# Loading one of the last rows in six strided parts instead of five, meant to give the DMA engines 10, 9, 7 and 6 of its partitions

## The chip, the cores and the metric

The kernel runs on one core of a Trainium2 chip. The metric is the device time of one execution in microseconds (us). A trace, where one is quoted, is of one execution; "from the start" means from the start of its span. The kernel before took 162.47 us (median of 3 runs, 162.40 to 163.06).

## The reference

A log-sum-exp over the last axis of a 32 x 512 x 1024 array of float32:

```
x_max = np.max(x, axis=-1, keepdims=True)
return x_max.squeeze(-1) + np.log(np.sum(np.exp(x - x_max), axis=-1))
```

There are 16,384 rows of 1024 numbers, 67.1 MB to read and 64 KB to write. The kernel takes exp without subtracting the maximum, sums, and takes the logarithm. "Row" below means one row per partition: 128 x 1024 numbers, 512 KB. There are 128 such rows.

## The kernel before

The rows arrive in 17 loads, from 16 rows down to single ones. ScalarE takes exp of each load; VectorE sums most of them, ScalarE some with its own accumulator. The last four loads (13 to 16) are one row each and ScalarE sums all of them.

```
CHUNKS = [                       # rows, rows summed by VectorE, pieces, by halves
    (4, 4, 1, False), (15, 15, 1, False), (16, 16, 2, False), ...
    (5, 4, 1, True), (4, 3, 1, True), (3, 3, 1, False), (2, 2, 1, True),
    (1, 0, 1, False), (1, 0, 1, False), (1, 0, 1, False), (1, 0, 1, False),
]
UNEVEN = (13,)
PARTS = ((0, 128, 2), (1, 128, 4), (3, 128, 8), (7, 64, 8), (71, 128, 8))
...
        if i not in UNEVEN:
            nc.sync.dma_start(out=dst, in_=src).then_inc(landed[i], 16)
            return
        for first, last, step in PARTS:
            nc.sync.dma_start(
                out=dst[first:last:step], in_=src[first:last:step]
            ).then_inc(landed[i], 16)
...
        for j in range(n_dve, r):                    # rows that ScalarE sums
            nc.scalar.activation(out=ring[:, s + j], in_=ring[:, s + j], func=Exp,
                accum_out=total(row + j)).then_inc(act_done, 1)
```

Load 13, the row four from last, is thus fetched in five parts, each a strided set of partitions: 0, 2, 4, ...; 1, 5, 9, ...; and so on. Just ahead of the final row ScalarE also takes the logarithm of 43 finished sums.

The softmax here doesn't subtract the row's maximum and nothing guards it: scores larger than these inputs give would overflow.

## Time and profile before

| | kernel before |
|---|---|
| time, median of 3 | 162.47 us |
| bytes read, mean rate over the span | 67.11 MB, 417 GB/s |
| DMA queue, share of 16 engines' span | 97.4% |
| last update of the semaphores of loads 12 to 16, from the start | 153.03, 154.62, 155.68, 156.98, 158.22 us |
| first to last update of load 12; of load 16 (the stagger) | 0.68; 0.56 us |

A semaphore is a counter; ScalarE waits in the kernel until a full load has brought it to 16. The trace records 16 updates for such a load, each with its time, and the load has landed with the last of them. The page counts 16 DMA engines, and below each update is read as the end of one engine's share. That is the author's reading: no record of the trace gives an engine's number. The page and the chain tell which engine is busy; these records tell how close each wait is, also where no idle time is printed. The lines of the profile themselves are in the prediction.

### The profile page before, as it was taken

To read this page: it belongs to the slowest core of one execution; us is meant where nothing else is said; L and a number is where in the kernel's file an instruction comes from. 1 tells how busy PE (TensorE), PEld (TensorE's weight loads), DVE (VectorE), ACT (ScalarE), POOL (GpSimd) and SP (SyncE) were. 2 spreads that over 40 slices of the span, in tenths; PEclk is the share of its full clock that TensorE was granted. 3 is DMA by queue.
4 is the path that set the end of the run, shared out by engine and by line. 5 is a ranking of instruction groups with operands and counts; after the bars stand their busy time and mean duration, and the time that the engine had idled before them with its cause. 6 is when DMAs were issued, how large, how long until landed. Compare 5 with 4: busy or idle time off the path is not lost.

```text
span 161.2 us, 130 instructions
## 1 busy us (share of the span) xinstructions
DVE 121.0 (75%) x46; ACT 115.2 (71%) x40; POOL 0.2 (0%) x4
## 2 busy tenths in 40 slices
DVE  0028000003999999999999699999999999999891
ACT  3170006996089960999429993999199999999995
POOL 0000000000000000000000000000000000000000
DMA  7999799989989989989979999999999999999991
GB/s 256 508 488 442 335 442 520 407 374 520 423 358 520 423 358 520 423 358 520 423 325 455 455 455 439 423 423 423 404 412 439 455 427 406 426 423 421 405 386 49
DMA packets 2640, 67.18 MB, mean 417 GB/s; under 512 B 336, under 2 KB 464, under 8 KB 976
## 3 DMA queue, kind: packets, MB, share of 16 engines
q1 hardware_dynamic: 2640, 67.18, 97.4%
HBM read 67.11 MB, written 0.07 MB: 417 GB/s over the span
## 4 chain that ended last, share of the span: by engine, by line
DMA 49%; DVE 29%; ACT 20%; issue 1%
DMA ring<-in_x_dram 49%; DVE sums L168 29%; ACT ring L148 17%; ACT ring L175 3%; ACT res L119 0%
## 5 line engine op out<-in xcount | busy, mean ns | idle before, releaser
L168 DVE TENSOR_REDUCE sums<-ring 128x8 f32<-128x8192 f32 (+5 forms) x14 | 111.2, 7995 | 37.0 <-ACT ring L148 36.9
L148 ACT ACTIVATE ring<-ring 128x8192 f32<-128x8192 f32 (+6 forms) x18 | 104.4, 5837 | 43.6 <-DMA ring<-in_x_dram 43.5
L155 DVE CUSTOM_DVE_ANT_0 ring<-ring 128x512 f32<-128x512 f32 x16 | 9.9, 688 | 0.0
L175 ACT ACTIVATE ring<-ring 128x1024 f32<-128x1024 f32 x9 | 9.3, 1045 | 0.0
L133 ACT ACT_TABLE_LOAD x1 | 1.3, 1283 | 0.8 <-PEq L220 0.8
L175 ACT ACTIVATION_READ_ACCUMULATOR ring<-ring 128x1 f32 x9 | 1.6, 175 | 0.0
L155 DVE DVE_READ_ACCUMULATOR2_ANT sums<- 128x1 f32 x16 | 1.3, 84 | 0.0
L119 ACT ACTIVATE res<-sums 128x81 f32<-128x81 f32 (+1 forms) x2 | 0.5, 251 | 0.0
L119 ACT ACTIVATE res<-late 128x4 f32<-128x4 f32 x1 | 0.2, 174 | 0.0
L220 POOL MEMSET const-uint8-127<- 128x1 uint8 x1 | 0.1, 103 | 0.0
L220 POOL MEMSET const-bfloat16-1.0<- 128x1 bf16 x1 | 0.1, 102 | 0.0
L220 POOL MEMSET const-float32-0.0<- 128x1 f32 x1 | 0.1, 99 | 0.2 <-issue 0.2
L220 POOL MEMSET const-float32-1.0<- 128x1 f32 x1 | 0.1, 99 | 0.0
## 6 DMA issues: line engine op xcount, KB each, us to landing
ring<-in_x_dram SPq DMA_DIRECT2D x1, 7680.0 KB, 24.9
ring<-in_x_dram SPq DMA_DIRECT2D x1, 7168.0 KB, 28.6
ring<-in_x_dram SPq DMA_DIRECT2D x1, 6656.0 KB, 35.7
ring<-in_x_dram SPq DMA_DIRECT2D x1, 4608.0 KB, 20.2
ring<-in_x_dram SPq DMA_DIRECT2D x2, 2048.0 KB, 16.1
ring<-in_x_dram SPq DMA_DIRECT2D x1, 3584.0 KB, 28.3
ring<-in_x_dram SPq DMA_DIRECT2D x1, 2560.0 KB, 27.3
ring<-in_x_dram SPq DMA_DIRECT2D x1, 1536.0 KB, 28.0
```

The lines of the kernel that those rows point to most:

```text
L119: nc.scalar.activation(out=res[:, lo:hi], in_=src, func=Ln).then_inc(act_done, 1)
L133: nc.scalar.preload_act_table_set("natural_log_exp_and_others")
L148: nc.scalar.activation(out=ring[:, s + lo : s + hi], in_=ring[:, s + lo : s + hi], func=Exp).then_inc(act_done, 1)
L155: nc.vector.tensor_tensor_reduce(out=ring[:, s + j, : D // 2], in0=ring[:, s + j, : D // 2], in1=ring[:, s + j, D // 2 :], scale=1.0, scal ...
L168: nc.vector.reduce_sum(out=sums[:, row + lo : row + hi], in_=ring[:, s + lo : s + hi], axis=AX).then_inc(dve_done, 1)
L175: nc.scalar.activation(out=ring[:, s + j], in_=ring[:, s + j], func=Exp, accum_out=total(row + j),).then_inc(act_done, 1)
L220: nc = _bacc.Bacc("TRN2", target_bir_lowering=False, num_devices=1)
```

## The change

The updates of a load come one after another, those of load 12 within 0.68 us. The intent is to give the engines that are ahead more of one row, so that all finish the last loads together and the last landing comes earlier. The kernel before was meant to do it in two halves (9 and 7 partitions an engine), the change in four quarters (10, 9, 7, 6), by cutting the third part, 16 partitions, in parts of 12 and 4. Which engine moves which partitions is assumption.

```diff
-PARTS = ((0, 128, 2), (1, 128, 4), (3, 128, 8), (7, 64, 8), (71, 128, 8))
+PARTS = (
+    (0, 128, 2), (1, 128, 4), (3, 96, 8), (99, 128, 8), (7, 64, 8), (71, 128, 8),
+)
```

Nothing else changes; the program is the same up to the issue of this row at 128 us. Line numbers below the edit grow by two.

## The prediction

> **What bounds the kernel now.** I read the page first (busy shares, then the chain of work that ended last), then the chain in order of time, then the timeline of the last microseconds, and last a table of stretches.
>
> ```profile
> span 161.2 us, 130 instructions
> DVE 121.0 (75%) x46; ACT 115.2 (71%) x40; POOL 0.2 (0%) x4
> q1 hardware_dynamic: 2640, 67.18, 97.4%
> DMA 49%; DVE 29%; ACT 20%; issue 1%
> ```
>
> The DMA queue is moving packets during 97.4% of the span, and neither compute engine is over 75%. The kernel reads 67.11 MB once, so in bulk it is a stream of loads. What sets the end, though, is the last stretch, which the averages do not tell.
>
> ```profile
> 122.15 24.68 DMA ring<-in_x_dram
> 146.83 0.02 issue
> 146.85 2.77 ACT ring L148
> 149.62 1.04 ACT ring L175 x2
> 150.66 4.46 ACT ring L148 x2
> 155.12 3.02 ACT ring L175 x6
> 158.14 0.13 ACT res L119
> 158.27 0.00 ACT ring L175
> 158.27 0.94 issue
> ```
>
> The reader is to see that after 146.85 us the chain names no transfer any more: it is ScalarE, one row after another, to the end. The row that the change touches is the first of the final four; ScalarE takes each with one 128x1024 activation and its own sum. The timeline shows them:
>
> ```profile
> 155.03 1.04 ACT L175 ACTIVATE ring<-ring 128x1024 f32<-128x1024 f32 x1
> 156.03 1.05 ACT L175 ACTIVATE ring<-ring 128x1024 f32<-128x1024 f32 x1
> 157.03 1.05 ACT L175 ACTIVATE ring<-ring 128x1024 f32<-128x1024 f32 x1
> 158.03 0.24 ACT L119 ACTIVATE res<-sums 128x43 f32<-128x43 f32 x1
> 158.25 1.06 ACT L175 ACTIVATE ring<-ring 128x1024 f32<-128x1024 f32 x1
> ```
>
> Each row starts 1.00 us after the one before, with no idle time printed. Against this I set when the rows landed, from the trace's records of semaphore updates (16 per full transfer[...]; the last one opens the row). From the span's start the last updates of the four rows are at 154.62, 155.68, 156.98 and 158.22 us. ScalarE begins them at 155.03, 156.03, 157.03 and 158.25. So the slack of the transfers is 0.41, 0.35, 0.05 and 0.03 us: **the two streams end almost together.** The last row may even be a wait on its transfer: an earlier logarithm starts at 127.92 and the activation behind it at 128.09, 0.17 us later, while here the distance is 158.25 - 158.03 = 0.22 us. Without any wait for data the last row would have begun at about 158.20. Hence at most **0.05 us** can be won by landing the last rows earlier, and anything over some 0.03 us of delay is lost one for one.
>
> The uneven row is visible as a dip of the rate:
>
> ```profile
> 149.90:152.40 2.50, 2.49 (x10) 2.50 (x3) 0.00 (x0) 1.00 0.99 410
> 153.20:154.60 1.40, 1.25 (x1) 1.40 (x2) 0.00 (x0) 1.00 1.04 337
> 154.60:157.10 2.50, 2.50 (x2) 2.50 (x6) 0.00 (x0) 1.00 1.01 403
> ```
>
> The last two columns are the DMA engines' busy share and GB/s. The engines are as busy in the middle stretch, but move 337 GB/s, not 403 to 410; the 4096-byte packets take up to some 245 ns there, against 159 ns before and after, in the packet records. The five strided parts of this row cost about 1.4 x (1 - 337/410) = 0.25 us of streaming.
>
> [...]the row's semaphore has 66 records, two of them (131.54 and 132.20 us) just after the issues of the 8-partition parts.[...]
>
> **The change, part by part.** [...]all else stays, instruction for instruction on ScalarE and VectorE.
>
> 1. *Issue.* One more issue on SyncE's queue. The five cost 567 to 664 ns, median 592, so the next three rows are issued 0.6 us later, at 132.4 instead of 131.8 us. They land 24 to 25 us after their issue because the queue is full ahead of them. Effect on the end: 0.
>
> 2. *Bytes.* [...]One packet is 0.16 us[...].
>
> 3. *What it does to the last landing.* An ordinary load before this row lands over 152.35 to 153.03 us, a stagger of 0.68 us; after it the stagger is 0.54, and for the last row 0.56 us (157.66 to 158.22). The trace gives no engine numbers. I choose to assume that the stagger follows them: engines 0 to 3 first. The last row's sixteen updates are 157.66, .79, .87, .92; .98, 158.02, .03, .06; .07, .07, .16, .17; .18, .18, .21, .22. Adding 0.175 to the first four gives 157.83 to 158.10, taking 0.16 off the last four gives 158.02 to 158.06, the middle eight stay, and the last is now 158.17: 0.05 us earlier, and the stagger falls to some 0.2 to 0.35 us.
>
> 4. *What ScalarE makes of it.* It would begin the last row at 158.20 instead of 158.25. Sum: 0 + 0 - 0.05 = **-0.05 us**, 0.03% of 162.47.
>
> **Rivals.** *The skew is balanced the wrong way.* If one of the last engines in the list is among 0 to 3[...], its final landing goes from 158.22 to about 158.40, and the end moves by +0.15 us: about 162.6.[...] The dip costs 0.25 us now; if it grew by half the end would come 0.1 us later, if it shrank by half the landing would gain 0.12 us, of which ScalarE lets through only 0.05. *ScalarE hides it entirely.* If the last row was not waiting on data, the change is worth 0.00. *The new issue starves the queue*: it would take 20 us of delay, not 0.6; I give it nothing.
>
> **Range and chances.** The favourable end is cut off at -0.05 us; the unfavourable rivals give +0.1 to +0.2 us. Beside these stand the run-to-run differences of the kernel before, 162.40 to 163.06 us in three runs, which are larger than everything above. I expect 162.45 us, with 162.2 to 162.8 holding eight times in ten. Two per cent is 3.2 us, sixty times the gain that can be had and more than ten times the largest loss I can construct, so within 2% gets 0.98 and either side 0.01.
>
> **What would show it.** In the changed kernel's trace: the row's semaphore should have 64 + 4 = 68 records; six issues near 128.6 to 132.4 us; the stagger of the final row below 0.45 us; its last update between 158.1 and 158.2 us, and ScalarE's final activation about 0.17 to 0.2 us behind the logarithm of 43 columns, all relative to the same start of the stream. ScalarE's work from 116 us on should keep its durations. The prediction is wrong if the last update comes later than 158.3 us, if the stagger grows, or if the stretch of the uneven row falls well below 337 GB/s. A difference that lies before 128 us has nothing to do with the change.

The sum came to 0 + 0 - 0.05 = -0.05 us, and its last term, step 3, is an estimate on the assumption that the change gives four engines one packet more and four one packet less. A packet is 0.16 us in the trace before (159 ns), and 0.175 is that and 0.015 for a 4-byte packet of a semaphore update (9 ns there) with a gap. The count of 64 + 4 = 68 updates can be checked in the trace.

## The result, and the profile after

| | before | after |
|---|---|---|
| median, same rounds | 162.56 us (6 runs, 162.37 to 163.06) | 162.84 us (6 runs, 162.76 to 162.91) |
| ratio, 95% interval | | 1.0012 [0.9995, 1.0029]: the same at 2% |
| last updates of loads 12, 13, 14, 15, 16 | 153.03, 154.62, 155.68, 156.98, 158.22 | 153.20, 154.95, 156.04, 157.32, 158.56 |
| last landing of 12 to last landing of 16 | 5.19 us | 5.36 us |
| stagger of load 16 | 0.56 us | 0.66 us |

A ratio here is the mean time of one kernel's fast runs over that of the other's of the same rounds, so not quite the ratio of the medians.

The page of the changed kernel: the span, the busy times, the queue and the shares of the chain.

```profile
span 161.5 us, 131 instructions
DVE 121.0 (75%) x46; ACT 115.4 (71%) x40; POOL 0.2 (0%) x4
q1 hardware_dynamic: 2640, 67.18, 97.3%
DMA 48%; DVE 33%; ACT 13%; SPq 3%; issue 1%
```

The busy times and their shares are as they were; one more instruction is the sixth issue. The chain now holds 3% of SyncE's queue. In order of time (start, duration, what), its end is:

```profile
128.41 0.56 SPq L113
...
131.85 0.57 SPq L113
132.42 0.04 issue
132.47 0.44 SPq L108
132.91 0.04 issue
132.95 24.38 DMA ring<-in_x_dram
157.32 0.02 issue
157.35 0.81 ACT ring L177
```

The six issues stand in the chain only because a wait of ScalarE is now found at 157.32 us, for load 15, and the chain is followed from there back to that load's issue. The 24.38 us between issue and landing are the queue ahead of it (its packets take 97.3% of 16 engines' span), so the issues are not what cost anything. What matters is that the chain meets a transfer at 157.32, where before the last transfer in it ended at 146.83. ScalarE's own lines show both waits:

```profile
155.20 1.04 ACT L177 ACTIVATE ring<-ring 128x1024 f32<-128x1024 f32 x1
156.20 1.04 ACT L177 ACTIVATE ring<-ring 128x1024 f32<-128x1024 f32 x1
157.35 1.06 ACT L177 ACTIVATE ring<-ring 128x1024 f32<-128x1024 f32 x1
158.36 0.23 ACT L121 ACTIVATE res<-sums 128x43 f32<-128x43 f32 x1
158.59 1.06 ACT L177 ACTIVATE ring<-ring 128x1024 f32<-128x1024 f32 x1
```

The third row starts 1.15 us after the second, where the others follow at 1.00: 0.15 us of waiting for a landing at 157.32. The last starts 0.23 us after the logarithm, 0.02 us after its landing at 158.56. No idle time is printed for gaps as small as these; one sees them in the starts. The three stretches that the prediction shows, now of the changed kernel (last column GB/s):

```profile
149.90:152.40 2.50, 2.44 (x8) 2.50 (x3) 0.00 (x0) 1.00 0.98 413
153.20:154.60 1.40, 1.07 (x1) 1.40 (x2) 0.00 (x0) 1.00 1.06 310
154.60:157.10 2.50, 2.50 (x2) 2.50 (x4) 0.00 (x0) 1.00 1.01 405
```

The stretch of the strided row moves 310 GB/s instead of 337, with the engines just as busy (DMA share 1.06 against 1.04); ahead of it and behind it the rates are as before.

Of the 0.34 us between the two spans (161.18 and 161.52), 0.17 us are there at load 12 already, where the two programs are still the same. Over the twelve traces whose loads up to 12 come in undisturbed, that landing lies anywhere from 152.88 to 153.43 us, so this part is chance. The other 0.17 us lies behind it, and the experiments are about that part.

### The profile page after: what moved, and what is told of

Read it like the earlier page. It is cut to its first block, busy times and chain, and to the rows that moved or that the text cites. A ratio compares the mean times of both kernels' runs of the same rounds, so it can differ in the third digit from the quotient of the medians.

```text
span 161.5 us, 131 instructions
## 1 busy us (share of the span) xinstructions
DVE 121.0 (75%) x46; ACT 115.4 (71%) x40; POOL 0.2 (0%) x4
## 2 busy tenths in 40 slices
DMA packets 2640, 67.18 MB, mean 416 GB/s; under 512 B 336, under 2 KB 464, under 8 KB 976
## 3 DMA queue, kind: packets, MB, share of 16 engines
q1 hardware_dynamic: 2640, 67.18, 97.3%
## 4 chain that ended last, share of the span: by engine, by line
DMA 48%; DVE 33%; ACT 13%; SPq 3%; issue 1%
DMA ring<-in_x_dram 48%; DVE sums L170 33%; ACT ring L150 12%; SPq L113 2%; ACT ring L177 1%; SPq L108 0%; ACT res L121 0%
```

## The experiments

**How they are measured.** A few tenths of a us out of 162 are near what repeated times can resolve, so the verdicts rest on distances inside each trace. Three are used. The *delay of the mean*: the mean of the sixteen updates of load 16, less the mean for load 12. By estimate a skew that adds as many bytes to some engines as it takes from others does not move this mean in first order, while lost streaming does. The *lag of the last*: last update of load 16 less their mean; this is what a skew is to reduce. And the *last landing*: last of load 16 less last of load 12. The last update already lags behind the mean at load 12, by 0.27 to 0.47 us from trace to trace before the programs differ, so lags of different traces cannot be set side by side as they are. The last landing less the delay of the mean is the change of the lag between load 12 and load 16 of one trace, and that can be compared: -0.17 and -0.19 us in the two traces of the kernel before, -0.03 in plain. Where the parts of row 13 disturb load 12 itself (halves, six97), the mean of load 11 is the reference; a plain load then gives 7.59 us. Each variant has one trace; only the two kernels have more, and their repeats differ by up to 0.02 us (before) and 0.05 us (changed) in the delay of the mean.

| run | parts of the row (partitions an engine as meant, not traced) | delay of mean from 12; from 11 | lag of last | last landing | ratio of times to before |
|---|---|---|---|---|---|
| plain | one load | 5.10; 7.59 | 0.44 | 5.07 | 0.9996 |
| columns2 | 2, by columns | 5.17; 7.67 | 0.32 | 5.16 | 0.9995 |
| even4 | 4, 8 an engine | 5.33; 7.82 | 0.41 | 5.30 | 1.0009 |
| skew9887 | 5, 9-8-8-7 | 5.31; 7.81 | 0.19 | 5.24 | 1.0006 |
| kernel before | 5, 9-9-7-7 | 5.37; 7.86 | 0.19 | 5.19 | |
| before_again | the same | 5.35; 7.84 | 0.26 | 5.16 | 1.0009 |
| changed kernel | 6, 10-9-7-6 | 5.48; 7.97 | 0.29 | 5.36 | 1.0012 |
| after_again | the same | 5.46; 7.95 | 0.18 | 5.27 | 1.0015 |
| after_third | the same | 5.43; 7.92 | 0.23 | 5.33 | 1.0015 |
| swapped | 6, other order | 5.47; 7.96 | 0.25 | 5.42 | 1.0010 |
| six97 | 6, 9-9-7-7 | 5.84; 8.61 | 0.20 | 5.53 | 1.0036 |
| halves | 2, by partitions | 6.10; 8.87 | 0.67 | 6.02 | 1.0097 |
| before3 | 5, on three rows | 6.43; 8.92 | 0.50 | 6.60 | 1.0080 |
| after3 | 6, on three rows | 6.27; 8.76 | 0.81 | 6.70 | 1.0083 |

**Theory**: strided parts cost streaming; the change makes this a little dearer and gains no lag in return. (The author's reason, that engines get in each other's way, no trace shows.) **Rival 1**: extra bytes make the engines that get them the last ones (lag grows, mean stays). **Rival 2**: the number of issues and semaphore packets costs. **Rival 3**: the difference is chance.

### Repeats: after_again, after_third, before_again

No edit; the two kernels, again.

> The changed kernel once more, to see what repeats. Measured inside the trace from the last landing of the two-row load ahead of the strided row to the last landing of the final row: 5.36 us in the first trace, against 5.19 us before. Theory (the six parts cost more streaming, and the last engine is no earlier): 5.3 to 5.4 us again, time within 0.3 us of the kernel before. Rival (the first trace was a chance state of the engines' stagger): 5.1 to 5.25 us, and no difference in time.

> The changed kernel a third time, on the same chip as the last three. If the 0.1 us of extra mean delay is real it comes out at 5.42 to 5.52 us again, and the ratio of times at 1.0005 to 1.002; if it was chance, the mean falls to 5.3 to 5.4 us, or the ratio to 1.000 and below.

> The kernel before, submitted as a candidate, so that it leaves a second trace and a null comparison. Ratio 1.000, with an interval that shows what this comparison can resolve (about 0.001 to 0.002). Same distance in the trace: 5.15 to 5.25 us if it repeats; if it comes out at 5.3 us or more, the difference of the first two traces is chance.

after_again: 163.01 us against 162.69, ratio 1.0015 [1.0002, 1.0028]. after_third: 162.74 against 162.56, 1.0015 [1.0, 1.003]. before_again, which compares a kernel with itself: 162.68 against 162.69, ratio 1.0009 [0.9989, 1.0029]. So the times alone can hardly tell 0.2 us from nothing. The traces can, if few of them: last landing 5.36, 5.27 and 5.33 us in three traces of the change, 5.19 and 5.16 in two of before; delay of the mean 5.43 to 5.48 against 5.35 and 5.37, so 0.10 us more on average (5.457 - 5.36). after_again missed its range: its distance, 5.27 us, lies between the theory's (5.3 to 5.4) and the rival's (5.1 to 5.25), and its time 0.32 us above that of the kernel before, not within 0.3. The lag of the last fell by 0.12, 0.19 and 0.10 us in the changed kernel and by 0.17 and 0.19 in the kernel before. Of the 0.14 us by which the last landing is later on average, 0.10 are thus in the mean and 0.04 in a lag that fell less; the second part is smaller than the scatter of the repeats. Rival 3 is unlikely for the landing, since all three traces lie above both of before (but see after3 below), and Rival 1 explains at most the smaller part.

### plain: no strided parts

```diff
-UNEVEN = (13,)
+UNEVEN = ()
```

> No strided row at all: the row goes in one 128-partition load[...]. If strided parts cost streaming (0.2 us in the kernel before, 0.35 to 0.4 in the changed one), the distance is 4 rows x 1.24 = 4.96 us and the mean landing comes earlier by as much, while the stagger stays at 0.68 us. If instead the uneven split pays for itself, the last landing is no earlier than before's 5.19. In time ScalarE caps the gain: 0.0 to -0.1 us against the kernel before on either reading.

The plain kernel's middle stretch, where the strided row dipped to 337 and 310 GB/s, is this:

```profile
153.20:154.60 1.40, 1.17 (x1) 1.40 (x2) 0.00 (x0) 1.00 1.03 413
```

No dip is left. The mean comes 0.26 us earlier than in the kernel before (5.10 against 5.37 and 5.35), but the lag of the last falls by only 0.03 us from load 12 on, where the five parts bring it down by 0.18, so the last landing is only about 0.1 us earlier (5.07; 4.96 was expected from 1.24 us a row, but a row takes 1.28 here). ScalarE then runs free at the end:

```profile
157.10 1.05 ACT L175 ACTIVATE ring<-ring 128x1024 f32<-128x1024 f32 x1
158.09 0.24 ACT L119 ACTIVATE res<-sums 128x43 f32<-128x43 f32 x1
158.24 1.04 ACT L175 ACTIVATE ring<-ring 128x1024 f32<-128x1024 f32 x1
```

The last row follows the logarithm after 0.15 us, with its data there since 158.18. From the activation of load 12 to that of load 16 it is 4.94 us here, 5.02 and 4.99 in the kernel before, 5.18, 5.10 and 5.15 in the changed one. So what this trace wins against before is 0.05 to 0.08 us. In time: 162.62 us against 162.69, ratio 0.9996 [0.9983, 1.0009]. **The strided parts of the kernel before earn nothing against a plain load**: they bring the last update 0.18 us nearer to the mean and put the mean back by 0.26.

The packet records show where the 0.26 us goes. The last four rows are 512 packets of 4096 bytes in all these kernels. Their durations, summed and divided by the 16 engines, make 5.21 us with the plain load, 5.42 with even4, 5.41 with skew9887 (both below), 5.47 and 5.46 in the two traces of the kernel before, and 5.57, 5.51 and 5.52 in those of the changed kernel. The packets are not more, they take longer while the strided row passes: up to 172 ns in that stretch with the plain load, up to 255 in the kernel before and 298 in the changed one (first trace of each).

### even4: strided, but meant as 8 partitions an engine

```diff
-PARTS = ((0, 128, 2), (1, 128, 4), (3, 128, 8), (7, 64, 8), (71, 128, 8))
+PARTS = ((0, 128, 2), (1, 128, 4), (3, 128, 8), (7, 128, 8))
```

> The row in four strided parts of 64, 32, 16 and 16 partitions[...]. If the cost lies in the strided parts[...], the mean landing is late by 0.1 to 0.25 us against the plain load and the stagger stays near 0.68. If the cost of the changed kernel lies in the bytes of engines 0 to 3, this run shows no delay of the mean against plain. Time within 0.2 us of before.

```profile
153.20:154.60 1.40, 1.12 (x1) 1.40 (x2) 0.00 (x0) 1.00 1.03 345
```

The dip is back (345 GB/s) although no skew is meant. The mean is 0.23 us later than with the plain load, the lag stays at 0.41. So most of the cost of the uneven row, 0.23 of 0.26 us, comes with strided parts even when they are meant to give every engine the same number of bytes. The time was 162.78 us against 162.69, ratio 1.0009 [0.9994, 1.0024].

### columns2 and halves: two parts each, by columns and by partitions

```diff
# columns2
-PARTS = ((0, 128, 2), (1, 128, 4), (3, 128, 8), (7, 64, 8), (71, 128, 8))
+PARTS = ((0, 512), (512, 1024))
-        for first, last, step in PARTS:
+        for lo, hi in PARTS:
-                out=dst[first:last:step], in_=src[first:last:step]
+                out=dst[:, :, lo:hi], in_=src[:, :, lo:hi]
# halves
+PARTS = ((0, 64, 1), (64, 128, 1))
```

> Control for the number of parts: the row in two loads of all 128 partitions by 512 columns[...]. If issues and semaphore packets cost nothing, mean delay against plain below 0.08 us[...] and no dip of the rate; if the splitting itself costs, 0.1 us or more.

> The row in two contiguous parts of 64 partitions[...], no stride, only two issues. If the number of parts (issues, semaphore packets) makes the cost, the mean delay against plain is at most 0.1 us. [...]it is as large as with four strided parts (0.23 us) or larger, and the rate dips to 340 GB/s or below in the stretch.

(The last sentence of the second text: the figures to be met if the cost does not hang on the number of parts.)

The middle stretch of columns2:

```profile
153.20:154.60 1.40, 1.30 (x1) 1.40 (x2) 0.00 (x0) 1.00 1.04 413
```

and of halves:

```profile
153.20:154.60 1.40, 1.23 (x1) 1.11 (x2) 0.00 (x0) 1.00 1.05 246
```

Both have two issues and load the same 512 KB. By columns the mean moves by 0.07 us and the rate stays at 413 GB/s. By partitions the engines are as busy (DMA share 1.05, plain 1.03), but the rate falls to 246 (in the 0.8 us just before, 152.4 to 153.2 us, to 205, where plain has 410), load 12 itself is held up (its updates spread over 1.36 us) and the mean, from load 11, is 8.87 - 7.59 = 1.28 us late. A single row streams in 1.28 us (plain, mean of load 12 to mean of load 13), so the row took twice its time. The rate, 205 against 410 GB/s, is half. What is shown is that the cost hangs on which partitions go together in a part, and not on the number of parts; where the packets are held up no trace shows. One thing is left untested: the rows of neighbouring partitions lie 512 KB apart in the input, so each of these edits also changes which addresses are read together, and no run keeps the reads and changes the writes alone. The times: columns2 162.43 against 162.59 us, ratio 0.9995 [0.9971, 1.0018]; halves 164.22, ratio 1.0097 [1.0075, 1.0119].

### six97: six parts, meant to keep the old bytes an engine

```diff
-PARTS = ((0, 128, 2), (1, 128, 4), (3, 128, 8), (7, 64, 8), (71, 128, 8))
+PARTS = ((0, 64, 2), (64, 128, 2), (1, 128, 4), (3, 128, 8), (7, 64, 8), (71, 128, 8))
```

> Six parts like the changed kernel[...]: the part of 64 is cut in two of 32. So far the mean landing of the final row lies 5.36 us after that of the two-row load with the five parts (two traces: 5.37, 5.35), 5.47 with the changed six (5.48, 5.46), 5.10 with a plain load. If the sixth part as such costs the 0.1 us: 5.45 to 5.5. If it is which engine writes which partitions at which moment: anything else, 5.2 to 5.4 or above 5.55. Time within 0.3 us of before.

```profile
153.20:154.60 1.40, 1.36 (x1) 1.21 (x2) 0.00 (x0) 1.00 0.99 255
```

It was to be a control for the sixth part and failed as one: each of its two first parts stays in one half of the partitions, like halves, and it paid like halves: 255 GB/s, the mean 8.61 - 7.59 = 1.02 us late from load 11, time 163.22 against 162.56 us (within 0.3 was expected), ratio 1.0036 [1.0023, 1.005]. It says nothing about a sixth part, but that where a part lies weighs far more than one part more.

### skew9887: a 16 cut in 12 and 4, meant as little skew

```diff
-PARTS = ((0, 128, 2), (1, 128, 4), (3, 128, 8), (7, 64, 8), (71, 128, 8))
+PARTS = ((0, 128, 2), (1, 128, 4), (3, 128, 8), (7, 96, 8), (103, 128, 8))
```

> Five parts of 64, 32, 16, 12 and 4 partitions[...]. Strided parts[...] left the last engine 0.41 us behind the mean (plain 0.44), the five parts of before 0.18 and 0.26, the six of the change 0.29 and 0.18. If the skew is what pulls the last engine in, this one lies between, 0.25 to 0.35 us behind the mean; the mean itself near 5.36 us (five parts). Time within 0.3 us of before.

This is even4 with its last part of 16 cut in 12 and 4, the very kind of cut that the change makes. The mean is 5.31 us, against 5.33 for even4: **here the cut and the issue it adds cost nothing that can be seen**, so Rival 2 falls for one cut of this kind (the page counts 2640 packets, 336 of them under 512 B, for the kernel before and for the changed one, so the sixth part adds no packet). The lag of the last is 0.19 us where 0.25 to 0.35 was expected. That is not the skew's doing: in this trace the lag was 0.27 us at load 12 already, the smallest of all, and fell by 0.08, which lies between plain (0.03) and the five parts (0.17, 0.19). So the lag falls by more with the parts meant as 9-9-7-7 than with those meant as 9-8-8-7, and by no more with those meant as 10-9-7-6 (0.05 to 0.19, swapped included). The time was 162.64 against 162.56 us, ratio 1.0006 [0.9991, 1.0021].

### swapped: the part of four issued last

```diff
-PARTS = ( ..., (3, 96, 8), (99, 128, 8), (7, 64, 8), (71, 128, 8) )
+PARTS = ( ..., (3, 96, 8), (7, 64, 8), (71, 128, 8), (99, 128, 8) )
```

> The changed kernel's six parts[...], with the part of 4 partitions issued last instead of fourth. If the bytes per engine and the number of parts decide, mean 5.45 to 5.5 us and last landing 5.2 to 5.4 as in the changed kernel.[...] Time within 0.3 us of before.

The mean is 5.47 us, as in the changed kernel (5.43 to 5.48): the place of the part of four in the order does not matter. The last landing, 5.42, came just above what was expected (5.2 to 5.4), since the lag fell by only 0.05 us. The time: 162.75 against 162.56 us, ratio 1.0010 [0.9998, 1.0022].

### before3 and after3: both schemes on three rows

```diff
-UNEVEN = (13,)
+UNEVEN = (13, 14, 15)
```

once with the five parts, once with the six.

> The kernel before's five parts on three of the last four rows, so that their cost shows in the time and not in the trace alone. From the first traces one such row delays the mean landing of the final row by 0.26 us against a plain load; three should give 0.8 us[...]. Expected: last landing 6.3 to 6.5 us after that of the two-row load (one strided row: 5.2), time +1.0 to +1.3 us against before. If the parts are free and only the skew counts: +0.3 us.

> The changed kernel's six parts on the same three rows. Mean delay 3 x 0.37 = 1.1 us[...]. Expected: last landing 6.9 to 7.2 us after that of the two-row load, time +1.6 to +2.0 us against before, so 0.5 to 0.8 us over the run with five parts on three rows. If the difference of the two schemes is chance, the two runs agree within 0.3 us.

A term, 0.48 and 0.95 us for rows that some engines would carry beyond the mean: the expected last landings, 6.3 to 6.5 and 6.9 to 7.2 us, contain it.

ScalarE in before3 and then in after3; the bracket is the idle time ahead of the instruction, and what ended it:

```profile
157.07 1.06 ACT L175 ACTIVATE ring<-ring 128x1024 f32<-128x1024 f32 x1 [0.66 <-DMA ring<-in_x_dram]
158.98 1.06 ACT L175 ACTIVATE ring<-ring 128x1024 f32<-128x1024 f32 x1 [0.79 <-DMA ring<-in_x_dram]
```

```profile
156.66 1.06 ACT L175 ACTIVATE ring<-ring 128x1024 f32<-128x1024 f32 x1 [0.58 <-DMA ring<-in_x_dram]
158.77 1.06 ACT L175 ACTIVATE ring<-ring 128x1024 f32<-128x1024 f32 x1 [0.99 <-DMA ring<-in_x_dram]
```

Here the waits are plain, and they cost time: before3 163.92 us against 162.59, ratio 1.0080 [1.0056, 1.0105]; after3 164.02, ratio 1.0083 [1.0064, 1.0102]. So strided rows at the end cost real time, as the theory has it, and more than foretold for the five parts: the mean of before3 is 1.33 us behind plain's, where 0.8 was expected, its last landing 6.60 (6.3 to 6.5), its time 1.33 us over before (1.0 to 1.3). after3 came below its ranges, with 6.70 (6.9 to 7.2) and 1.43 us (1.6 to 2.0). The step from five to six parts did not grow with the number of rows: after3 was to be 0.5 to 0.8 us slower than before3 and was 0.1. Its mean is even earlier (6.27 against 6.43 us), and only its lag larger (0.81 against 0.50), as Rival 1 would have it. By the rule set down beforehand (within 0.3 us of each other) this pair speaks for chance. There is one trace of each, and before3's is of the slowest of its four executions (164.44 us). So the 0.10 us that the change adds to the mean of one row is no fixed price per row; with one row it came back in every trace.

## Why the prediction was right or wrong

- **Right: the time hardly moves, within 2%.** Three comparisons gave 1.0012, 1.0015 and 1.0015. The first median, 162.84 us, lies 0.04 us above the top of the range (162.8), the later ones, 163.01 and 162.74, on either side of it. The sign of the small expected step was wrong. That the class came true says little for the working: 2% is 3.2 us, and all runs, halves with 1.0097 too, are the same by that measure.
- **Right: two streams that end together, with next to nothing to win** (0.05 us at most, it said; 0.05 to 0.08 by the plain trace). The last row did wait for its transfer, so the rival "ScalarE hides it entirely" falls. With the plain load the last row began 0.15 us behind the logarithm, where 0.17 had been read off an earlier pair, and ScalarE's stretch shrank by 0.05 to 0.08 us.
- **Right: step 1, the issue.** The six issues took 4.01 us in SyncE's queue and the row's semaphore has the 68 records foretold, four of them (130.88, 131.60, 132.24 and 132.85 us) just behind the issues of the parts of 12, 4, 8 and 8. In skew9887 such an extra cut was free.
- **Wrong: step 3, what it does to the last landing.** It said "the last is now 158.17: 0.05 us earlier, and the stagger falls to some 0.2 to 0.35 us". The last update came at 158.56 us; less the 0.17 us that the run was behind at load 12, it is 0.17 us later, not 0.05 earlier. Over all traces: 5.32 us on average behind load 12 against 5.18, so 0.14 us later. The stagger was 0.66, 0.38 and 0.56 us. The step shifted sixteen updates by packets of 0.16 us and held everything else still. In the runs the packets of the row took longer, by 0.07 us an engine, and the mean came 0.10 us later; and the lag fell by 0.04 us less than before instead of further. The assumption that the engines finish in the order of their numbers, with the rows dealt out as meant, is not borne out either: shifts of +2, +1, -1 and -2 packets of 0.16 us on the updates of load 12, dealt out in that order, would leave a stagger of 0.28, 0.31 and 0.36 us (an estimate for the three traces) where 0.66, 0.38 and 0.56 were measured. By the signs that the prediction itself had named it was wrong here: the last update came after 158.3 us, and in the first trace the stagger grew and the rate fell to 310 GB/s. The longest packets of the row, too, are longer than it read off: 255 ns, not 245.
- **The rivals of the prediction.** That the dip itself changes comes nearest: the rate dipped to 310 GB/s, in the repeats to 331 and 319, against 337 and 339 in the two traces of before, and the mean came 0.10 us later, where it had said an end 0.1 us later for a dip grown by half. "The skew is balanced the wrong way" had the right total (+0.15 us), but its reason, a last engine with more bytes, accounts for 0.04 us at most.
- **Step 4 in reverse.** A later landing is passed on by ScalarE one for one once its slack of 0.03 to 0.05 us is gone: its stretch from load 12 to load 16 grew from 5.00 to 5.14 us on average.

**What stays open.** Why the packets take longer still with the six parts. It is not an issue more as such (skew9887), not the order of the part of four (swapped), and not a price per row (after3). Engine numbers are not in the trace, and no run tells whether the packets are held up where they are written or where they are read.

No variant beats the kernel before clearly. The plain load, which is simpler, is level with it.

## What to carry to other kernels

Before evening out a stagger by hand, measure what the uneven transfer itself costs: here the strided parts cost 0.26 us of streaming to bring the last update 0.18 us nearer to the mean, and a finer split cost 0.10 us more and brought the last update no nearer. Where two streams end almost together, as the loads and ScalarE do here, look at both: landing the rows earlier alone won hardly anything (0.05 to 0.08 us with plain), and slowing the loads lost in full (landings 0.14 us later on average with the change, ScalarE's stretch 0.14 us longer). Distances inside a trace, between a landing ahead of the change and one behind it, resolve a tenth of a microsecond that the times of whole runs do not; a lag is to be compared with the lag of the same trace ahead of the change.

## What was measured of the transfers

- The row in two partition halves landed 1.28 us later (mean), one more row's time, at 246 GB/s; in two column halves 0.07 us later, at 413.
- With parts of every second, fourth and eighth partition, meant to spread evenly over the engines (even4), the mean landing of the last row came 0.23 us later and the rate dipped to 345 GB/s.
- This core read at 417 GB/s on average over its whole span.
- The sixteen updates of one ordinary load, up to load 12, come 0.61 to 0.84 us apart from first to last in the first traces of the two kernels, and the spread is carried from load to load (0.66, 0.67, 0.68 us for loads 10, 11 and 12 of the kernel before).
